# Expert biases as stacked one-pass matmuls, and the scatter of expert rows as a one-hot matmul of gated, split rows

## The chip, the cores and the metric

The kernel runs on one core of a Trainium2 chip. The metric is the time of one execution on the device in microseconds. The core has five engines with instruction streams of their own: TensorE (PE; its weight loads are shown as PEld), VectorE (DVE), ScalarE (ACT), GpSimd (POOL) and SyncE (SP), which here mostly issues DMAs. They meet through semaphores only.

## What is computed

Two transformer blocks, one after the other, on 256 tokens of 1024 channels, all in float32. Only the end of the first block is touched: a mixture of 32 experts, of which each token takes 4. Some 400 of the 486 MB that the kernel moves are expert weights. Cut to what matters:

```python
def moe_ffn(h, w_router, b_router, w1, b1, w2, b2):
    logits = hf @ w_router + b_router
    top_val, top_idx = lax.top_k(logits, TOP_K)        # 4 of 32
    gates = jax.nn.softmax(top_val, axis=-1)
    ...                                                # rows of each expert collected
    def expert_block(args):
        e, tok, g = args
        xb = hf[tok]
        gu = xb @ w1[e] + b1[e]                        # 1024 -> 2048
        gate = jnp.minimum(gu[:, :D_FF], SWIGLU_LIMIT)
        up = jnp.clip(gu[:, D_FF:], -SWIGLU_LIMIT, SWIGLU_LIMIT)
        act = (up + 1.0) * gate * jax.nn.sigmoid(SWIGLU_ALPHA * gate)
        return (act @ w2[e] + b2[e]) * g[:, None]      # 1024 -> 1024, times the gate
    ...                                                # summed back per token
```

## The kernel before, in words

**Stages.** From 0 to about 229 us the first block's mixing and memory attention run (`block_pre`); its weight matmuls (L319) take operands split by ACT (L209, the rounded high part `wh`) and DVE (L210, the rest `wl`). From about 229 to 1212 us the experts run one after the other (`block_moe`). From there `post_head` and the second block take the rest.

**One expert.** Each expert has 64 slots. `gather` (L714) collects the rows of four experts at a time with a one-hot matrix `OG`. `expert_in` then computes 64 x 2048 values as four outputs of 64 x 512 in two PSUM banks, the halves of a bank in the left and right 64 columns of the array. First come four bias matmuls (L741): a one-hot `bs` of 32 rows (L736, DVE) picks row e of the bias table `b1`, whose four quarters lie in four groups of 32 partitions. Then 32 matmuls follow (L746), four for each of eight weight chunks. A float32 matmul is two instructions on the chip. DVE and ACT make the activation (L808 to L812), PE transposes it (L815), ACT copies it out (L817), and 16 matmuls (L829) over four weight chunks make the output `Y`, 64 rows for each half of the channels, which lie in partitions 0 to 63 and 64 to 127.

**Combine.** After every second expert, `combine` adds two experts' rows back to the tokens `x`. `weigh` (L788) has multiplied the one-hot by the gates, so `combine_weights` transposes gated one-hots (L800, copied by ACT at L802), each twice, for the two halves of partitions. `rows_out` copies `Y` to `ysb` (L834, ACT). Eight float32 matmuls with 64 rows each (L845) and four additions by DVE (L848) finish it. For the last two experts `post_head` does the same at L1084, and at L1109 it adds the same product in transposed form to a transposed copy of `x` (L884), which the next block needs.

**Order and buffers.** A scheduler builds each engine's order ahead of time; every engine then runs its list in order. The weights come in 1 MB chunks, issued by SP in the order of use: for each expert eight of `w_expert_in` (L198) and four of `w_expert_out` (L201). Twelve buffers named `w` hold them. SP's next issue waits until PE (or whoever read it last) has released the buffer. At expert 16 (`half`) there is a branch (L868, L869) that handles experts with more than 64 tokens and isn't taken with these inputs; weights for some chunks are loaded ahead of it.

Of the kernel before, what the change touches and what calls it, by code (L numbers as in the profile page):

```python
# [10 lines left out]
F32 = mybir.dt.float32  # L11
F32R = mybir.dt.float32r
# [4 lines left out]
ALU = mybir.AluOpType  # L17
# [25 lines left out]
def host_constants():  # L43
    i = np.arange(P)
    f = np.float32
    c = {}
    c["ident"] = np.eye(P, dtype=f)
    c["ones"] = np.ones((P, P), f)
    c["sbtri"] = -(i[:, None] >= i[None, :]).astype(f)
    c["nones"] = -np.ones((P, P), f)  # L50
    c["neg"] = np.where(i[:, None] >= i[None, :], f(-1e30), f(0))
    c["before"] = (i[:, None] < i[None, :]).astype(f)
    c["iota_e"] = np.tile(np.arange(NE, dtype=f), (P, 1))
    c["iota_s"] = np.tile(np.arange(CAP, dtype=f), (P, 1))
    c["bselc"] = np.concatenate([np.eye(NE, dtype=f)] * 4)
# [12 lines left out]

WIDTH = {"iota_e": NE, "iota_s": CAP, "bselc": NE, "omask": 64}
# [273 lines left out]
def block_pre(K, A):  # L343
# [92 lines left out]
    moe_load(K, A)  # L436
    K.gemm(w_in, 1024, 4, xT, "N", ev_vu, pre=pre_w)
# [140 lines left out]
    ple_load(K, A)  # L578
    ssx2 = K.t([P, 2, 4], F32, "ssx", 2)
# [178 lines left out]
def block_moe(K, A, x):  # L758
# [73 lines left out]
    def rows_out(e):  # L832
        y = K.t([P, 512], F32, "ysb", 3)
        nc.scalar.copy(y, Ys.pop(e))  # L834
        return y

    def combine(e):
        cws = [combine_weights(e - 1), combine_weights(e)]
        ys = [K.yprev, rows_out(e)]
        for tt in range(2):  # L840
            pss = [K.bank("A") for _ in range(2)]
            for i in range(2):
                for h in range(2):
                    pr = slice(64 * h, 64 * h + 64)
                    nc.tensor.matmul(pss[h], cws[i][pr, tt], ys[i][pr], start=i == 0, stop=i == 1)  # L845
            for h in range(2):
                xs = x[:, tt, h * 512:(h + 1) * 512]
                nc.vector.tensor_tensor(xs, pss[h], xs, op=ALU.add)  # L848
# [4 lines left out]
    for e in range(K.nexp):  # L853
# [17 lines left out]
        if prev is not None:  # L871
            gemm2(e - 1, prev, ahead2, range(LAST if last else 0, 4))
# [14 lines left out]
    K.cw, K.Y = cw, Ys[last]  # L887
# [164 lines left out]
def post_head(K, A, x):  # L1052
# [4 lines left out]
    y = K.t([P, 512], F32, "ysb", 3)  # L1057
# [645 lines left out]
def program(tc, A, cst, out, nexp=NE, post=True):  # L1703
    with ExitStack() as ctx:
# [7 lines left out]
        bias_in(K, A)  # L1712
# [67 lines left out]
```

## Time and profile before

| what | us |
|---|---|
| median of 3 runs | 1556.54 |
| lowest and highest | 1555.26, 1558.83 |
| the profiled execution's own time | 1555.18 |
| its span (first to last instruction) | 1553.4 |
| PE busy, share of the span | 1470.1, 95% |
| DVE, ACT, POOL busy | 540.0, 384.1, 53.0 |
| bytes moved by DMA | 486.31 MB |

Busy shares are averages over stages. In the expert stage PE is busy nearly all the time and so is the DMA; in the second block both have gaps. A busy PE here includes weight loads and pipelined ends. PEclk is the clock that was granted to TensorE as a share of 2.4 GHz; 0.5 is 1.2 GHz. The DMA share is the mean of the core's 16 DMA engines.

### The profile page before, as it was taken

The page shows a single profiled execution, that of the slowest core. Times are in us where ns is not written, and L with a number is a line of the kernel's source. Part 1 is how long each engine was busy: PE and PEld are TensorE (multiplying, and loading weights), DVE is VectorE, ACT ScalarE, POOL GpSimd, SP SyncE. Part 2 cuts the span into 40 slices and gives each one's busy share as a digit, 9 for nine tenths or more (in the row PEclk, how much of TensorE's full clock was granted, in tenths as well). Part 3 has the DMA queues.
Part 4 walks back from the last instruction along what each step waited for, and adds up shares of the span by engine and source line. Part 5 has one row for each costly group of instructions (what it writes and reads, how often), then busy time and mean ns, then how long its engine had stood idle before and what let it go on. Part 6 is the DMA issues. An engine that isn't in the chain of part 4 may idle for free.

```text
span 1553.4 us, 20385 instructions
## 1 busy us (share of the span) xinstructions
PE 1470.1 (95%) x8440; PEld 797.7 (51%) x8440; DVE 540.0 (35%) x993; ACT 384.1 (25%) x783; POOL 53.0 (3%) x56
## 2 busy tenths in 40 slices
PE   9999999999999999998999999999999975889998
PEld 7899983332333333332233333223333764878998
DVE  5557652112121111121111111211111655985575
ACT  5845441000010010010001000000000553445654
POOL 0010010000000000000000000000000102500000
PEclk9999999999999999999999999999999997999999
DMA  9694348999999999999999999999998453332463
GB/s 336 218 317 163 119 172 308 418 415 418 417 407 400 410 417 416 416 418 369 382 416 418 410 416 418 415 417 414 388 419 331 140 109 98 109 123 89 153 197 107
DMA packets 146497, 486.31 MB, mean 313 GB/s; under 512 B 8605, under 2 KB 77341, under 8 KB 113504
## 3 DMA queue, kind: packets, MB, share of 16 engines
q1 hardware_dynamic: 143968, 479.10, 79.1%
q0 software_dynamic: 1504, 4.12, 1.5%
q10 hardware_dynamic: 928, 1.74, 0.4%
q8 instruction: 68, 1.11, 0.3%
q14 instruction: 29, 0.24, 0.0%
HBM read 481.78 MB, written 3.15 MB: 312 GB/s over the span
## 4 chain that ended last, share of the span: by engine, by line
PE 38%; issue 7%; DVE 4%; DMA 2%; ACT 2%; POOL 0%; POOLq 0%; ACTq 0%; DVEq 0%
PE pP L746 13%; PE pY L829 9%; PE pA L319 4%; PE pA L845 3%; PE pP L741 3%; DMA w<-in_w_in_dram 2%; DVE t L1375 1%; PE pA L714 1%; PE pY L1320 1%; PE pA L815 1%; DVE t L1376 1%; DVE r L1369 1%; PE pP L1688 0%; PE pA L800 0%; DVE x L848 0%
## 5 line engine op out<-in xcount | busy, mean ns | idle before, releaser
L746 PE MATMUL pP<-w,xg 128*64 128x512 f32 x2024 | 444.0, 594 | 0.0
L746 PEld LDWEIGHTS pP<-w,xg 128*64 128x64 f32 x2024 | 143.2, 137 | 294.4 <-issue 278.7
L829 PE MATMUL pY<-w,hgu 128*64 128x512 f32 x1024 | 279.7, 614 | 4.6 <-PEq L869 4.6
L209 ACT CAST wh<-w 128x512 fp32r<-128x512 f32 (+1 forms) x256 | 155.1, 615 | 157.0 <-PE pA L319 97.4
L210 DVE TENSOR_TENSOR wl<-w,wh 128x512 fp32r<-128x512 f32 x232 | 157.0, 687 | 76.3 <-ACT wh L209 73.2
L808 DVE TENSOR_SCALAR wh<-pP 128x512 f32<-128x512 f32 x32 | 22.1, 691 | 445.4 <-PE pP L746 445.4
L829 PEld LDWEIGHTS pY<-w,hgu 128*64 128x64 f32 x1024 | 71.6, 138 | 160.6 <-issue 145.7
L809 ACT ACTIVATE wh<-wh 128x512 f32<-128x512 f32 x32 | 20.2, 630 | 518.4 <-DVE wh L808 500.0
L319 PE MATMUL pA<-wh,xh 128*128 128x256 f32 x496 | 143.4, 289 | 2.5 <-DVE bk L1346 2.5
L319 PE MATMUL pA<-wh,xl 128*128 128x256 f32 x496 | 142.6, 288 | 0.0
L319 PE MATMUL pA<-wl,xh 128*128 128x256 f32 x496 | 141.5, 285 | 0.0
L319 PE MATMUL pA<-xh,wh 128*128 128x256 f32 x368 | 107.6, 292 | 4.5 <-ACT wh L209 2.3
L319 PE MATMUL pA<-xh,wl 128*128 128x256 f32 x368 | 105.9, 289 | 2.3 <-DVE wl L210 2.3
L319 PE MATMUL pA<-xl,wh 128*128 128x256 f32 x368 | 104.7, 285 | 0.0
L319 PEld LDWEIGHTS pA<-wh,xh 128*128 128x128 f32 x496 | 95.9, 193 | 4.0 <-issue 3.1
L845 PE MATMUL pA<-ysb,cw 64*128 64x512 f32 x240 | 76.5, 654 | 21.5 <-DVE x L848 11.6
L319 PEld LDWEIGHTS pA<-wl,xh 128*128 128x128 f32 x496 | 95.6, 193 | 0.4 <-issue 0.2
L319 PEld LDWEIGHTS pA<-wh,xl 128*128 128x128 f32 x496 | 95.5, 193 | 0.3 <-issue 0.2
L848 DVE TENSOR_TENSOR x<-pA,x 128x512 f32<-128x512 f32 x60 | 38.8, 686 | 153.4 <-PE pA L845 153.4
L741 PE MATMUL pP<-b,bs 32*64 32x512 f32 x256 | 89.5, 617 | 0.0
L319 PEld LDWEIGHTS pA<-xh,wh 128*128 128x128 f32 x368 | 70.5, 192 | 7.7 <-ACT wh L209 3.4
L319 PEld LDWEIGHTS pA<-xh,wl 128*128 128x128 f32 x368 | 70.4, 192 | 3.5 <-DVE wl L210 3.1
(425 smaller groups left out, 1417.5 us busy)
## 6 DMA issues: line engine op xcount, KB each, us to landing
w<-in_w_expert_in_dram SPq DMA_DIRECT2D x253, 1024.0 KB, 11.8
w<-in_w_expert_out_dram SPq DMA_DIRECT2D x128, 1024.0 KB, 10.7
w<-in_w_in_dram SPq DMA_DIRECT2D x31, 1024.0 KB, 5.5
w<-in_w_mem_kv_dram SPq DMA_DIRECT2D x8, 1024.0 KB, 12.0
w<-in_w_out_dram SPq DMA_DIRECT2D x8, 1024.0 KB, 5.6
w<-in_w_mem_q_dram SPq DMA_DIRECT2D x4, 1024.0 KB, 7.0
w<-in_w_mem_o_dram SPq DMA_DIRECT2D x4, 1024.0 KB, 5.3
w<-in_w_ple_gate_dram SPq DMA_DIRECT2D x4, 1024.0 KB, 4.7
```

Of the source, the lines that this page charges most:

```text
L209: nc.scalar.copy(wh, src)
L210: (nc.gpsimd if lo == "P" else nc.vector).tensor_tensor(wl, src, wh.bitcast(F32), op=ALU.subtract)
L319: nc.tensor.matmul(ps[:, j], lh, rh, start=n == 0, stop=n == tot - 1)
L714: nc.tensor.matmul(ps, xx[tt][:, k * P:(k + 1) * P], og[:, tt], start=n == 0, stop=n == 3)
L741: nc.tensor.matmul(out[i], bs[pr], K.b1[pr], start=True, stop=False, tile_position=(32 * i, 64 * (i % 2)))
L746: nc.tensor.matmul(out[i], xs, raw[:, i * 512:(i + 1) * 512], start=False, stop=k == KT - 1)
L808: nc.vector.tensor_scalar(g, Pb[0], 7.0, None, op0=ALU.min)
L809: nc.scalar.activation(sg, g, AF.Sigmoid, scale=1.702)
L815: nc.tensor.transpose(ps[:, j].rearrange("p a b -> p (a b)"), u[:, j * P:(j + 1) * P], c["ident"])
L829: nc.tensor.matmul(Y[64 * h:64 * h + 64], act[:, k % 4, k // 4], raw[:, j * 1024 + h * 512:j * 1024 + h * 512 + 512], start=k == 0, stop=k ...
L845: nc.tensor.matmul(pss[h], cws[i][pr, tt], ys[i][pr], start=i == 0, stop=i == 1)
L848: nc.vector.tensor_tensor(xs, pss[h], xs, op=ALU.add)
```

## The change

Two representations change; the weights' matmuls L746 and L829 stay as they are.

- **Bias.** `b1` becomes 128 rows x 2 x 512 in fp32r: for each of the two PSUM banks, rows 0 to 63 hold the rounded quarters of the bias table and rows 64 to 127 what the rounding left. `bias_in` loads the table twice (eight DMAs instead of four) and is called earlier in the program; the new `bias_split` makes the two parts with two ACT copies and two DVE subtractions. `bs` becomes 128 x 128, still one-hot, and the four bias matmuls of an expert become two, 128 x 128 by 512, one for each bank.
- **Scatter.** `weigh` no longer repeats its result. `combine_weights` transposes the gated one-hot at half the width (64 columns instead of 128), makes a plain one-hot out of it (`is_gt`, DVE) that ACT copies to the upper 64 partitions, and sums up the gates (`reduce_sum`, DVE; copied up by ACT). It is now called for each expert at the place where its `gemm2` begins. `rows_out` no longer copies `Y`: for each half of the channels ACT multiplies it by the gate into one half of the partitions of `st`, rounded to fp32r, and DVE computes what the rounding left into the other half. The eight float32 matmuls with 64 rows become eight fp32r matmuls with 128 rows. `post_head` does the same for the last two experts.

The core of the diff:

```diff
 def bias_in(K, A):
-    b1 = K.b1 = K.m([P, 512], F32, "b1", 1)
-    for i in range(4):
-        nc.scalar.dma_start(b1[32 * i:32 * i + 32], A["b_expert_in"][0][:, 512 * i:512 * i + 512])
+    b1 = K.b1 = K.m([P, 2, 512], F32R, "b1", 1)
+    K.b1raw = [K.m([P, 512], F32, "ohr", 2) for _ in range(2)]
+    for b in range(2):
+        for i in range(4):
+            o = 1024 * b + 512 * (i % 2)
+            nc.scalar.dma_start(K.b1raw[b][32 * i:32 * i + 32], A["b_expert_in"][0][:, o:o + 512])
+def bias_split(K):
+    lo = slice(64, P)
+    for b, raw in enumerate(K.b1raw):
+        nc.scalar.copy(K.b1[:, b], raw)
+        nc.vector.tensor_tensor(K.b1[lo, b], raw[lo], K.b1[lo, b].bitcast(F32), op=ALU.subtract)
 def expert_in(K, A, e, spare={}):
-    for i in range(4):
-        pr = slice(32 * i, 32 * i + 32)
-        nc.tensor.matmul(out[i], bs[pr], K.b1[pr], start=True, stop=False, tile_position=(32 * i, 64 * (i % 2)))
+    for b in range(2):
+        nc.tensor.matmul(Pb[b], bs.rearrange("p j c -> p (j c)"), K.b1[:, b], start=True, stop=False)
     def combine_weights(e):
-        ps = K.bank("A", (P, 2, P))
-        for tt in range(2):
-            nc.tensor.transpose(ps[:, tt], OHG[g][:, tt, j].rearrange("p a b -> p (a b)"), c["ident"])
-        cw = K.t([P, 2, P], F32, "cw", 4)
-        nc.scalar.copy(cw, ps)
-        return cw
+        ps = K.bank("A", (CAP, 2, P))
+        for tt in range(2):
+            nc.tensor.transpose(ps[:, tt], OHG[g][:, tt, j], c["ident"])
+        cw = K.t([P, 2, P], F32R, "cw", 4)
+        gate = K.t([P, 1], F32, "gate", 4)
+        nc.vector.tensor_scalar(cw[0:64], ps, 0.0, None, op0=ALU.is_gt)
+        nc.scalar.copy(cw[64:P], cw[0:64].bitcast(F32))
+        nc.vector.reduce_sum(gate[0:64], ps, axis=AX.XY)
+        nc.scalar.copy(gate[64:P], gate[0:64])
+        return cw, gate
     def combine(e):
-        cws = [combine_weights(e - 1), combine_weights(e)]
-        ys = [K.yprev, rows_out(e)]
-        for tt in range(2):
-            pss = [K.bank("A") for _ in range(2)]
-            for i in range(2):
-                for h in range(2):
-                    pr = slice(64 * h, 64 * h + 64)
-                    nc.tensor.matmul(pss[h], cws[i][pr, tt], ys[i][pr], start=i == 0, stop=i == 1)
+        pair = K.yprev, rows_out(K, Ys.pop(e), cwg.pop(e))
+        for tt in range(2):
             for h in range(2):
+                ps = K.bank("A")
+                for i, (cw, st) in enumerate(pair):
+                    nc.tensor.matmul(ps, cw[:, tt], st[h], start=i == 0, stop=i == 1)
+def rows_out(K, Y, cwg):
+    cw, gate = cwg
+    st = []
+    for h in range(2):
+        t = K.t([P, 512], F32R, "st", NST)
+        a, b = (slice(64 * i, 64 * i + 64) for i in (h, 1 - h))
+        K.nc.scalar.mul(t[a], Y[a], gate[a])
+        K.nc.vector.scalar_tensor_tensor(t[b], Y[a], gate[a], t[a].bitcast(F32), op0=ALU.mult, op1=ALU.subtract)
+        st.append(t)
+    return cw, st
...
 def post_head(K, A, x):
-        nc.scalar.copy(y, K.Y)
-        for j in range(4):
-            for h in range(2):
-                k = 4 * h + j
-                pr = slice(64 * h, 64 * h + 64)
-                for i, yy in enumerate((K.yprev, y)):
-                    mm(K.xT[k // 2][:, k % 2], yy[pr, j * P:(j + 1) * P], K.cw[i][pr].rearrange("p a b -> p (a b)"),
-                       start=False, stop=k % 2 == 1 and i == 1)
+        pair = K.yprev, rows_out(K, K.Y, K.cwg)
+        for k in range(KT):
+            for i, (cw, st) in enumerate(pair):
+                mm(K.xT[k // 2][:, k % 2], st[k // 4][:, k % 4 * P:k % 4 * P + P], cw.rearrange("p a b -> p (a b)"),
+                   start=False, stop=k % 2 == 1 and i == 1)
```

The scheduler also builds another order. The first place is PE at a pair's second expert, between the last L746 (L761 in the changed kernel) of one expert and the first of the next. `pP` are the two banks of `expert_in`, `pY` the output bank, `pA` the banks of the transposes and the combine; a float32 matmul is one row here. Before:

```order
L741 MATMUL pP_5607<-b_397_2522,bs_5605 64x512 [waits DVE_49]
L741 MATMUL pP_5608<-b_397_2522,bs_5605 64x512 [waits DVE_49]
L829 MATMUL pY_5398<-w_5399,hgu_5298 64x512 [waits DMAHW7_49,Activation_49]
L829 MATMUL pY_5398<-w_5399,hgu_5298 64x512 x3
L800 MATMUL pA_5423<-cpack_120,ohw_4620 128x128 x2
L741 MATMUL pP_5608<-b_397_2522,bs_5605 64x512
L845 MATMUL pA_5435<-ysb_5325,cw_5426 128x512 [waits Activation_49]
L829 MATMUL pY_5398<-w_5417,hgu_5298 64x512 [waits DMAHW2_49]
L845 MATMUL pA_5435<-ysb_5433,cw_5431 128x512 [waits Activation_49]
L845 MATMUL pA_5443<-ysb_5325,cw_5426 128x512 [waits DVE_49]
L746 MATMUL pP_5453<-w_5459,xg_4575 64x512 [waits DMAHW3_49]
```

Now:

```order
L756 MATMUL pP_5734<-b_77_484,bs_5732 128x512 [waits DVE_49]
L756 MATMUL pP_5735<-b_77_484,bs_5732 128x512 [waits DVE_49]
L848 MATMUL pY_5520<-w_5521,hgu_5400 64x512 [waits DMAHW3_49,Activation_49]
L815 MATMUL pA_5511<-cpack_120,ohw_4710 64x128 x2
L857 MATMUL pA_5551<-st_5436,cw_5405 128x512 [waits Activation_49]
L857 MATMUL pA_5555<-st_5439,cw_5405 128x512 [waits DVE_49,PE_49]
L761 MATMUL pP_5569<-w_5573,xg_4665 64x512 [waits DMAHW7_49]
L857 MATMUL pA_5551<-st_5545,cw_5514 128x512 [waits DVE_49]
L857 MATMUL pA_5555<-st_5548,cw_5514 128x512 [waits DVE_49]
L857 MATMUL pA_5559<-st_5436,cw_5405 128x512 [waits DVE_49]
L857 MATMUL pA_5563<-st_5439,cw_5405 128x512 [waits DVE_49]
L761 MATMUL pP_5569<-w_5579,xg_4665 64x512 [waits DMAHW0_49]
```

The bias is one piece instead of two, and the last six combine matmuls now stand among the next expert's first four weight matmuls: L761 goes 1, 2, 1 and then 28 in a row, where L746 went 32 in a row behind the whole combine.

The second place is DVE at the same pair's end, where `st` is made and `x` is added to. Before, only the additions stood there:

```order
L736 CAST bs_5827<-cpack_120 128x64 [waits PE_49]
L848 TENSOR_TENSOR x_112<-pA_5435,x_112 128x512 [waits PE_49]
L848 TENSOR_TENSOR x_112<-pA_5436,x_112 128x512 [waits PE_49]
L848 TENSOR_TENSOR x_112<-pA_5443,x_112 128x512 [waits PE_49]
L848 TENSOR_TENSOR x_112<-pA_5444,x_112 128x512 [waits PE_49]
```

Now:

```order
L818 TENSOR_SCALAR cw_5514<-pA_5511 64x256 [waits PE_49]
L820 TENSOR_REDUCE gate_5515<-pA_5511 64x1
L909 SCALAR_TENSOR_TENSOR st_5545<-pY_5520,gate_5515,st_5545 64x512 [waits DVE_49,Activation_49]
L909 SCALAR_TENSOR_TENSOR st_5548<-pY_5520,gate_5515,st_5548 64x512 [waits Activation_49]
L859 TENSOR_TENSOR x_112<-pA_5551,x_112 128x512 [waits PE_49]
L859 TENSOR_TENSOR x_112<-pA_5555,x_112 128x512 [waits PE_49]
```

On ACT `rows_out` was one copy (L834). Before:

```order
L809 ACTIVATE wh_5385<-wh_5383 128x512 [waits DMAHW3_49,DMAHW0_49,DVE_49]
L817 COPY hgu_5396<-pA_5391 128x512 [waits PE_49]
L802 COPY cw_5426<-pA_5423 128x256 [waits PE_49]
L802 COPY cw_5431<-pA_5428 128x256 [waits PE_49]
L834 COPY ysb_5433<-pY_5398 128x512 [waits PE_49,Activation_49]
```

Now:

```order
L828 ACTIVATE wh_6546<-wh_6544 128x512 [waits DVE_49]
L836 COPY hgu_6557<-pA_6552 128x512 [waits PE_49]
L819 CAST cw_6562<-cw_6562 64x256 [waits DVE_49]
L821 COPY gate_6563<-gate_6563 64x1 [waits DVE_49]
L908 ACTIVATE st_6593<-pY_6568,gate_6563 64x512 [waits PE_49]
L908 ACTIVATE st_6596<-pY_6568,gate_6563 64x512 [waits DVE_49]
```

The copy became two multiplications by the gate. The second of them waits for DVE's first L909, so `rows_out` goes ACT, DVE, ACT, DVE, and DVE's one-hot, sum and split rows now come ahead of its additions.

The third place is ACT near the program's start, where the split of the biases is put between casts of the first weight matrix `w_in` (L211 is L209 of before). Before:

```order
L209 CAST wh_277<-w_113 128x512 [waits DVE_49,PE_49]
L209 CAST wh_295<-w_115 128x512 [waits DMAHW4_49,DVE_49,PE_49]
L209 CAST wh_311<-w_115 128x512 [waits DVE_49,PE_49]
L209 CAST wh_327<-w_115 128x512 [waits DVE_49,PE_49]
L209 CAST wh_343<-w_115 128x512 [waits DVE_49,PE_49]
```

Now:

```order
L211 CAST wh_277<-w_113 128x512 [waits DVE_49,PE_49]
L628 DMA ohr_486<-in_b_expert_in_dram 32x512
L211 CAST wh_295<-w_115 128x512 [waits DMAHW5_49,DVE_49,PE_49]
L211 CAST wh_311<-w_115 128x512 [waits DVE_49,PE_49]
L635 CAST b_77_484<-ohr_485 128x512 [waits DMAHW2_49,DMAHW0_49]
L211 CAST wh_327<-w_115 128x512 [waits DVE_49,PE_49]
L635 CAST b_77_484<-ohr_486 128x512 [waits DMAHW6_49,DMAHW7_49,DMAHW4_49,DMAHW1_49]
L211 CAST wh_343<-w_115 128x512 [waits DVE_49,PE_49]
```

The two bias casts stand behind the DMAs that they wait for, and the second of them stands ahead of five casts of `w_in`.

## Rows read from the trace of the kernel before

**Rows 1.** Windows: stretch, length, busy us of PE, PEld, DVE, ACT, POOL, PEclk, DMA, GB/s
```profile
260.00:1190.00 930.00, 901.60 (x3832) 300.09 (x3830) 154.70 (x263) 76.17 (x148) 0.00 (x0) 0.99 1.01 410
590.00:700.00 110.00, 106.97 (x456) 34.68 (x453) 18.50 (x30) 8.76 (x17) 0.00 (x0) 1.00 1.02 417
500.00:510.00 10.00, 10.00 (x49) 3.42 (x50) 0.82 (x2) 0.00 (x0) 0.00 (x0) 1.00 0.95 354
710.00:720.00 10.00, 10.00 (x48) 3.29 (x46) 0.00 (x0) 0.00 (x0) 0.00 (x0) 1.00 0.64 232
750.00:760.00 10.00, 10.00 (x47) 3.21 (x46) 1.29 (x2) 0.00 (x0) 0.00 (x0) 1.00 0.76 293
1110.00:1120.00 10.00, 8.87 (x30) 3.30 (x32) 2.67 (x4) 0.30 (x1) 0.00 (x0) 0.83 0.83 323
```

**Rows 2.** Waits of SP, whole span: engine, line, releaser, us, times, longest
```profile
SPq L198 <- PE pP L746: 403.2, 233, 9.5
SPq L201 <- PE pY L829: 300.4, 107, 10.6
```

**Rows 3.** Chain of waits, four experts: start us, us to the next, what
```profile
750.67 13.88 PE pP L746 x64
764.55 1.86 PE pP L741 x6
766.41 1.00 PE pY L829 x2
...
769.86 1.00 PE pP L741 x2
770.86 5.30 PE pY L829 x24
776.16 13.73 PE pP L746 x64
...
808.52 13.88 PE pP L746 x64
...
871.51 13.88 PE pP L746 x64
```

**Rows 4.** DVE timeline, 776 to 812 us: who holds the banks of the biases
```profile
789.08 0.69 DVE L808 TENSOR_SCALAR wh<-pP 128x512 f32<-128x512 f32 x1 [17.99 <-PE pP L746]
789.94 0.69 DVE L810 TENSOR_SCALAR wh<-pP 128x512 f32<-128x512 f32 x1 [0.17 <-PE pP L746]
```

**Rows 5.** Chain of waits in the second block's head: matmuls in fp32r, 256 columns
```profile
1217.48 1.63 PE pA L1078 x12
```

**Rows 6.** PE timeline, 225 to 300 us: the bias matmuls of an early expert
```profile
278.02 1.09 PE L741 MATMUL pP<-b,bs 32*64 32x512 f32 x8
```

**Rows 7.** Timeline, 728 to 752 us: the end of one combine, PE and DVE
```profile
746.18 1.13 PE L845 MATMUL pA<-ysb,cw 64*128 64x512 f32 x4 [0.74 <-ACT ysb L834]
747.34 1.29 DVE L848 TENSOR_TENSOR x<-pA,x 128x512 f32<-128x512 f32 x2 [10.03 <-PE pA L845]
```

**Rows 8.** SP timeline, 240 to 275 us: DMA issues
```profile
257.85 12.34 SPq L198 DMA_DIRECT2D w<-in_w_expert_in_dram  x8
```

**Rows 9.** DMA view, 1166 to 1206 us, in 40 slices of 1 us
```profile
GB/s 410 426 434 426 410 418 434 426 418 385 422 406 397 414 397 418 401 422 397 410 406 426 397 418 387 340 321 350 106 25 0 0 0 0 69 275 385 316 19 0
```

**Rows 10.** Timeline, 1201.5 to 1216 us: the experts' end and the next head
```profile
1212.16 0.58 ACT L1103 COPY ysb<-pY 128x512 f32<-128x512 f32 x1 [9.51 <-PE pY L829]
...
1212.80 2.96 PE L1109 MATMUL pP<-cw,ysb 64*128 64x256 f32 x24 [0.74 <-ACT ysb L1103]
```

**Rows 11.** ACT timeline, 0 to 60 us: casts of the first weights
```profile
31.24 2.36 ACT L209 CAST wh<-w 128x512 fp32r<-128x512 f32 x4 [3.86 <-DMA w<-in_w_in_dram]
```

**Rows 12.** PE timeline at the branch, and windows (as Rows 1) for the clock
```profile
732.20 1.94 PE L829 MATMUL pY<-w,hgu 128*64 128x512 f32 x2 [4.55 <-PEq L869]
...
220.00:230.00 10.00, 6.59 (x41) 5.42 (x41) 6.80 (x26) 5.70 (x13) 3.25 (x3) 1.00 0.32 105
730.00:740.00 10.00, 7.80 (x16) 2.05 (x16) 1.49 (x3) 0.74 (x2) 0.00 (x0) 0.53 1.00 415
```

More of the change, by code (lines that the diff above doesn't have):

```diff
@@ L54, in host_constants @@
     c["iota_s"] = np.tile(np.arange(CAP, dtype=f), (P, 1))
-    c["bselc"] = np.concatenate([np.eye(NE, dtype=f)] * 4)
+    eye = np.eye(NE, dtype=f)
+    none = np.zeros((NE, NE), f)
+    c["bselc"] = np.block([[eye, none], [none, eye], [eye, none], [none, eye]])
     band = np.zeros((P, 4, 3, P), f)
@@ L436, in block_pre @@
     moe_load(K, A)
+    bias_in(K, A)
     K.gemm(w_in, 1024, 4, xT, "N", ev_vu, pre=pre_w)
@@ L578, in block_pre @@
     ple_load(K, A)
+    bias_split(K)
     ssx2 = K.t([P, 2, 4], F32, "ssx", 2)
@@ L781, in block_moe @@
     OHG = {}
+    cwg = {}
     def weigh(g):
-        ow = K.t([P, 2, 4, 2, CAP], F32, "ohw", 2)
+        ow = K.t([P, 2, 4, CAP], F32, "ohw", 2)
         for tt in range(2):
-            gb = G[:, tt, 4 * g:4 * g + 4, None, None].to_broadcast([P, 4, 2, CAP])
-            og = K.OG[g][:, tt].bitcast(F32)[:, :, None, :].to_broadcast([P, 4, 2, CAP])
-            nc.vector.tensor_tensor(ow[:, tt], og, gb, op=ALU.mult)
+            gb = G[:, tt, 4 * g:4 * g + 4, None].to_broadcast([P, 4, CAP])
+            nc.vector.tensor_tensor(ow[:, tt], K.OG[g][:, tt].bitcast(F32), gb, op=ALU.mult)
         OHG[g] = ow
@@ L830, in gemm2 @@
                                      start=k == 0, stop=k == KT - 1)
[L832 to L835, printed above, removed]
     def combine(e):
-        cws = [combine_weights(e - 1), combine_weights(e)]
-        ys = [K.yprev, rows_out(e)]
+        pair = K.yprev, rows_out(K, Ys.pop(e), cwg.pop(e))
         for tt in range(2):
-            pss = [K.bank("A") for _ in range(2)]
-            for i in range(2):
-                for h in range(2):
-                    pr = slice(64 * h, 64 * h + 64)
-                    nc.tensor.matmul(pss[h], cws[i][pr, tt], ys[i][pr], start=i == 0, stop=i == 1)
             for h in range(2):
+                ps = K.bank("A")
+                for i, (cw, st) in enumerate(pair):
+                    nc.tensor.matmul(ps, cw[:, tt], st[h], start=i == 0, stop=i == 1)
                 xs = x[:, tt, h * 512:(h + 1) * 512]
-                nc.vector.tensor_tensor(xs, pss[h], xs, op=ALU.add)
+                nc.vector.tensor_tensor(xs, ps, xs, op=ALU.add)
     half = K.nexp // 2
@@ L871, in block_moe @@
         if prev is not None:
+            cwg[e - 1] = combine_weights(e - 1)
             gemm2(e - 1, prev, ahead2, range(LAST if last else 0, 4))
@@ L876, in block_moe @@
             else:
-                K.yprev = rows_out(e - 1)
+                K.yprev = rows_out(K, Ys.pop(e - 1), cwg.pop(e - 1))
         prev = act
     last = K.nexp - 1
-    cw = [combine_weights(last - 1), combine_weights(last)]
+    K.cwg = combine_weights(last)
     K.xT = [K.bank("P", (P, 2, T)) for _ in range(4)]
@@ L886, in block_moe @@
     gemm2(last, prev)
-    K.cw, K.Y = cw, Ys[last]
+    K.Y = Ys[last]
+def rows_out(K, Y, cwg):
[8 more added lines that the diff above has]
+    return cw, st
 def dense_rest(K, A, x, xh, xl, pos, G, iota_e, g_f):
@@ L1081, in spread @@
         ps = K.bank("Y")
-        pr = slice(64 * h, 64 * h + 64)
-        for i, yy in enumerate((K.yprev, y)):
-            mm(ps, K.cw[i][pr, tt], yy[pr], start=i == 0, stop=i == 1)
+        for i, (cw, st) in enumerate(pair):
+            mm(ps, cw[:, tt], st[h], start=i == 0, stop=i == 1)
         queue.append((ps, x[:, tt, h * 512:(h + 1) * 512]))
@@ L1102, in post_head @@
     with K.tc.manual_schedule(engines={nc.scalar.engine, nc.vector.engine}):
-        nc.scalar.copy(y, K.Y)
-        for j in range(4):
-            for h in range(2):
-                k = 4 * h + j
-                pr = slice(64 * h, 64 * h + 64)
-                for i, yy in enumerate((K.yprev, y)):
-                    mm(K.xT[k // 2][:, k % 2], yy[pr, j * P:(j + 1) * P], K.cw[i][pr].rearrange("p a b -> p (a b)"),
-                       start=False, stop=k % 2 == 1 and i == 1)
+        pair = K.yprev, rows_out(K, K.Y, K.cwg)
+        for k in range(KT):
+            for i, (cw, st) in enumerate(pair):
+                mm(K.xT[k // 2][:, k % 2], st[k // 4][:, k % 4 * P:k % 4 * P + P], cw.rearrange("p a b -> p (a b)"),
+                   start=False, stop=k % 2 == 1 and i == 1)
         split(0)
@@ L1711, in program @@
         x, lg, finish = block_pre(K, A)
-        bias_in(K, A)
         with route(K, x, lg, finish):
```

9 lines of the change are left out of this document (5 added, 4 removed).

## The prediction

> **What bounds the kernel now.** I read the windows first, because busy shares over the whole span say little. From 260 to 1190 us PE is busy 901.6 of 930 us, and the DMA moves 410 GB/s; in a long quiet stretch (590 to 700) it moves 417 GB/s at a share of 1.02 [rows 1]. Both look full, so the question is which one leads. The waits of SP answer half of it: SP waited 403.2 us for PE's L746 and 300.4 us for its L829 [rows 2], so every chunk is issued when PE gives a buffer back. The chain of waits answers the other half. Four experts, one round of plain, combining, plain with gather, combining, take PE 871.51 - 750.67 = 120.84 us [rows 3]. The DMA needs for their 48 chunks of 1.049 MB, at 417 GB/s, 50.3 / 0.417 = 120.7 us. That is a tie. PE leads only by what it lost elsewhere: after each loss it is behind and cannot catch up, and when it is more than the twelve buffers behind, the DMA runs dry. That is what the windows with 354, 293 and 323 GB/s show [rows 1].
>
> The end shows how far PE is behind. In the slices of 1 us the rate falls from about 400 to under 350 at 1191 and to 106 at 1194, with one chunk of the next stage among the last bytes [rows 9]; so the last expert chunk lands at about 1193. The last expert's output is read at 1212.16 [rows 10]. **PE ends 19 us after the weights were there.**
>
> **The bias, part by part.** Removed are two groups of L741, 1.86 and 1.00 us for each expert [rows 3]. In their place come two one-pass matmuls of 512 columns. Twelve fp32r matmuls of 256 columns take 1.63 us [rows 5], 0.136 each; for 512 I take twice that, 0.27. They must still wait for the same banks: DVE frees the first at 789.77 and the second at 790.63 [rows 4], while PE comes from L746 at 789.89 [rows 3]. So the second ends at about 790.95, 1.1 us after L746. That saves 2.86 - 1.1 = 1.75; the two small transposes that each expert now has cost about 0.25. **A plain expert saves 1.5 us**, with bounds of 0.75 (the new pair takes the 1.86 of the old larger group) and 2.1 (no wait for the bank).
>
> Row tiling is what this part gives up. Here the eight bias instructions of an early expert stand together and take 1.09 us [rows 6], against 2.86 in two pieces later on. The Trainium skill, "TensorEngine Tiling (Array Packing)", section "Theoretical Speedup", says that a contraction of at most 32 rows gains up to four times by tiles side by side; the early expert agrees, the later ones don't. By that rule the old bias was worth 1.09 and the change brings nothing there, so four experts would take 4 x 1.75 = 7.0 us more than I work out below, 119.0, still under the DMA's 120.7, and the first rival would get 0.25. I go by the pieces as they ran.
>
> **The combine, part by part.** A combining expert now takes 808.52 - 776.16 = 32.36 us and a plain one 25.49, so the combine costs 6.87 [rows 3]. Afterwards: eight passes at 0.27, 2.2. Two L761 stand alone between them; a lone float32 matmul takes 1.00 where one of a row takes 5.30 / 12 = 0.44 [rows 3], so 1.1 more. Six more changes between kinds of matmul, at the 0.15 by which two equal groups of L746 differ (13.88 and 13.73), 0.9. Then waits. `rows_out` becomes ACT, DVE, ACT, DVE: ACT takes 0.58 for 512 columns [rows 10], DVE 0.65 (half of 1.29), and a hand-over some 0.1 (PE's wait of 0.74 around the copy) [rows 7], so the first `st` is there 1.4 us and the second 2.8 us after `Y`. Behind L857's wait on PE stand the next expert's weight matmuls, and SP waits for those. But the L761 in between cover most: 1.00 of the first 1.4, and 0.27 + 0.9 of the second, leaving 0.6. The last four wait for DVE's additions; I take the 0.74 that PE waits there now [rows 7]. Sum 2.2 + 1.1 + 0.9 + 1.3 = 5.5, a saving of 1.4. The bounds: 2.7 with no waits, and a loss of 0.9 if the chain and the additions are not covered (3.6 of waits).
>
> **Four experts** save 2 x 1.5 + 2 x (1.5 + 1.4) = 8.8 us: PE needs 112.0, between 107 and 119.6. At every bound that is less than 120.7. **So the DMA becomes the bound, and PE can make up 8.7 us of arrears in each four experts.** The added work elsewhere is beside it: some 2 us on DVE and 1 us on ACT for each expert, engines that are busy 154.7 and 76.2 of 930 us [rows 1].
>
> **What the catch-up is worth.** (a) The DMA no longer runs dry: (417 - 354) / 417 of 10 us is 1.5, the window at 750 gives 3.0, that at 1110 gives 2.25, in all 6.7 us. The 4.4 us at 710 stay, since SP itself stops at the branch there [rows 1]. From the means, (417 - 410) / 417 of 930 is 15.6 us of loss, so up to 4 more lie in small pieces; I don't count them. (b) PE's tail behind the last chunk. What is left then is that chunk's four matmuls, 8 x 0.22 = 1.8, and some arrears from the previous expert's combine and the transposes: 3 to 4 us, I take 3.5 instead of 19, **-15.5**. Ends: 2 (PE waits for the last chunk) and 9 (half the arrears remain).
>
> **The rest.** At the experts' start the first release lets SP go on at 257.85 [rows 8], and ahead of it PE has four groups of bias matmuls of about 1.0 [rows 3, 6] that become a quarter of that; part of it was covered by the gather, so -1.5 (0 to -2.4), which the DMA keeps. At the program's start 0.26 MB more are loaded, 0.6 us, while the DMA is the bound, and ACT does two casts of 0.6 us behind the last bias DMA, ahead of five casts of `w_in`. The cover is the 3.86 us for which ACT waits at 31.24 [rows 11]; +1.0 (0 to +4, when the last bias chunk lands so late that the cover is gone). In `post_head` PE's 2.96 us of L1109 behind a copy [rows 10] become one pass each, but `st` comes at 2.8 instead of 0.64 after `Y`: I take 0 (-2 to +2). After that everything waits for `x` and moves as a whole.
>
> **Sum**: -6.7 - 15.5 - 1.5 + 1.0 = -22.7 on the profiled execution's 1555.18, which is 1532.5. The median of the runs lies 1.36 above that execution, so I predict **1534 us**.
>
> **Rivals.**
> *PE stays the bound* (chance 0.10). The saved matmuls are given back as waits: for that each combine has to wait 4.3 us more than I take, since two of them in four experts must eat 8.7 us. For it speaks that `rows_out` and the additions now form one long chain over three engines; against it, that the whole chain is 2.8 us long and has L761 beside it. Small gains at the start and the end remain: 1552 to 1558, likeliest 1555.
> *The clock falls* (0.07), and the time ends above before. At the branch PE stood idle for 4.55 us, and in the window around it the granted clock is 0.53, the level of 1.2 GHz for nearly all of it; in 220 to 230, with gaps in PE's work too, it stays 1.00 [rows 12]. Once the DMA leads, PE waits for chunks all the time. If it then worked at 1.2 GHz for a share f of its work, four experts would take 112 x (1 + f), and that passes the 120.84 of today at f = 0.08. At f = 0.15 it is 128.8, and over some 7.5 rounds that makes +60 us, less 5 us of the start and end: about 1610. At f = 0.09 it is +9, less 5: about 1560. Against it speaks that it feeds on waits: as soon as PE falls behind, it has no wait left, so the rounds should settle at the DMA's 120.7. The worst that I then see is a fall in the last expert, +5 us, which the range holds. The Trainium skill, "TensorE: Matmul & The Clock Gate", section "HAM oscillation — how this bites in real kernels", describes a kernel that does just that, its clock falling in each wait for DMA between bursts of matmuls; the branch agrees with it, and no row here shows it in the short waits for a chunk.
> *The start is late* (0.08). The last bias DMA lands behind several chunks, ACT and DVE hold the casts of `w_in` for all of 4 us or more, and the catch-up ends at 9 us of tail: -6.7 - 10 + 4 + 2 = -10.7, about 1546.
> *More than I count* (0.10): the 4 us of small pieces, the earlier start and a shorter head: 1524 to 1529.
>
> **How the numbers follow.** My forecast, the DMA as the bound with PE 2 to 9 us behind at the end, has 0.65 and runs from 1528 to 1542. The late start and the larger gain are of the same sign. A measurement of this kernel tells about 0.2% (3.1 us) from no change. Faster: 0.65 + 0.08 + 0.10 = 0.83, plus 0.02 of the first rival, 0.85. Same: 0.07 of the first rival. Slower: 0.07 of the clock and 0.01 of the first. For 8 in 10 the range takes the forecast, the larger gain and most of the late start: 1525 to 1548.
>
> **What would show it.** Right: the starts of L761 over four experts lie about 120.7 apart and PE waits for chunks of `w_expert_in`; SP's waits for L761 and L848 shrink; the windows after 500 hold 417 except at the branch; from the last chunk's landing to the first ACT multiplication of `rows_out` in `post_head` there are 2 to 5 us. The bias pair ends about 1.1 us after L761, and L857's waits sum to about 1.3 us a combine. Wrong: PE without waits for DMA and rounds of 120.8 or more (first rival), PEclk well under 1.00 in many windows (the clock), or a first stage that ends over 3 us later. The number is wrong too if the second block does not move along as a whole.

## The result

The changed kernel takes **1531.83 us** (median of 4 runs, 1531.24 to 1534.87) beside 1555.9 of the kernel before in the same job: a ratio of **0.985** (95% interval 0.983 to 0.987). The forecast was 1534, with a range of 1525 to 1548. The profiled execution has a span of 1529.5 us, 23.9 less than before.

The windows of the changed kernel, with the columns of [rows 1]:

```profile
260.00:1170.00 910.00, 850.95 (x3546) 288.50 (x3544) 215.84 (x383) 105.60 (x208) 0.00 (x0) 1.00 1.01 414
500.00:510.00 10.00, 10.00 (x48) 3.52 (x46) 2.15 (x5) 1.79 (x4) 0.00 (x0) 1.00 1.03 423
710.00:720.00 10.00, 7.75 (x32) 2.30 (x28) 1.91 (x5) 1.11 (x3) 0.00 (x0) 1.00 0.65 242
730.00:740.00 10.00, 8.61 (x40) 2.26 (x34) 0.00 (x0) 0.00 (x0) 0.00 (x0) 1.00 1.01 413
750.00:760.00 10.00, 8.33 (x35) 1.94 (x32) 1.50 (x2) 1.36 (x2) 0.00 (x0) 1.00 1.01 421
880.00:890.00 10.00, 7.77 (x34) 1.94 (x32) 0.00 (x0) 0.00 (x0) 0.00 (x0) 1.00 1.01 418
1110.00:1120.00 10.00, 8.89 (x40) 2.74 (x38) 1.55 (x3) 1.64 (x4) 0.00 (x0) 1.00 1.02 422
```

PE now has gaps (7.77 us of 10 in a stretch of L761 alone), and the windows that held 354, 293 and 323 GB/s in [rows 1] hold 421 to 423. Only the stop at the branch is still there, 242 at 710. The waits of SP over the whole span (engine and line, whom it waited for, us, times, longest) changed hands:

```profile
SPq L203 <- DMA w<-in_w_expert_in_dram: 223.1, 113, 3.2
SPq L200 <- DMA w<-in_w_expert_out_dram: 213.3, 109, 3.3
SPq L200 <- PE pP L761: 138.2, 86, 7.2
...
SPq L203 <- PE pP L761: 46.4, 26, 4.2
```

In [rows 2] SP waited 403.2 and 300.4 us for PE to give buffers back. Now it mostly waits for an earlier transfer to land, and for PE's L761 only 138.2 + 46.4 = 184.6. (SP's waits for DVE's `wl`, of the other stages' weight matmuls, are left out: some 310 us in either kernel.) The chain of waits (start, us, what) runs through the transfers:

```profile
800.85 1.96 PE pP L761 x8
...
841.24 19.90 DMA w<-in_w_expert_in_dram
861.22 20.10 DMA w<-in_w_expert_in_dram
881.38 20.14 DMA w<-in_w_expert_out_dram
901.58 19.90 DMA w<-in_w_expert_in_dram
921.52 1.96 PE pP L761 x8
```

Where [rows 3] was PE throughout, five sixths of a round of four experts are now DMA pieces of about 20 us; the first 20 us, of which one line is shown, run over PE's work of one expert. The round takes 921.52 - 800.85 = 120.67 us: the DMA's 120.7. The next one, with two DMA pieces of 21.05 and 20.57 us in it, takes 122.28. So a round is hardly shorter than PE's 120.84 of before: what the change gains is the DMA's dry stretches and PE's tail at the end. The end, from the timeline (answering to [rows 10]; a bracket holds the us for which the engine stood idle before, and whom it waited for):

```profile
1183.12 5.37 PE L848 MATMUL pY<-w,hgu 128*64 128x512 f32 x24
1188.54 0.68 ACT L908 ACTIVATE st<-pY,gate 64x512 fp32r<-64x512 f32 x1 [6.93 <-PE pY L848]
1189.26 0.74 DVE L909 SCALAR_TENSOR_TENSOR st<-pY,gate,st 64x512 fp32r<-64x512 f32 x1 [6.85 <-ACT st L908]
1190.04 0.68 ACT L908 ACTIVATE st<-pY,gate 64x512 fp32r<-64x512 f32 x1 [0.81 <-DVE st L909]
1191.56 1.65 PE L1128 MATMUL pP<-cw,st 128*128 128x256 f32 x6 [0.30 <-DVE st L909]
```

`Y` is read at 1188.54 instead of 1212.16. The last expert chunk lands at 1184.93 (before: 1193.18, both from the transfers' own records), so PE's tail behind it fell from 19.0 to 3.6 us. From the first read of `Y` to the end of the program it is 341.0 us, before 341.2.

### The profile page after: what moved, and what is told of

Read it like the earlier page. It is cut to its first block, busy times and chain, and to the rows that moved or that the text cites. A ratio compares the mean times of both kernels' runs of the same rounds, so it can differ in the third digit from the quotient of the medians.

```text
span 1529.5 us, 19893 instructions
## 1 busy us (share of the span) xinstructions
PE 1414.1 (92%) x8104; PEld 788.1 (52%) x8104; DVE 606.0 (40%) x1123; ACT 416.4 (27%) x849; POOL 53.0 (3%) x56
## 4 chain that ended last, share of the span: by engine, by line
DMA 25%; PE 15%; issue 7%; DVE 5%; ACT 2%; POOL 0%; POOLq 0%; SPq 0%; DVEq 0%; ACTq 0%
DMA w<-in_w_expert_in_dram 14%; DMA w<-in_w_expert_out_dram 8%; PE pA L321 4%; PE pY L848 4%; PE pP L761 2%; DMA w<-in_w_in_dram 2%; DVE t L1394 2%; PE pA L730 1%; DVE t L1395 1%; PE pY L1339 1%; DVE r L1388 1%; PE pP L1707 0%; ACT wh L211 0%; PE pP L896 0%; DVE wl L212 0%
## 5 line engine op out<-in xcount | busy, mean ns | idle before, releaser
L761 PE MATMUL pP<-w,xg 128*64 128x512 f32 x2024 | 487.9, 598 | 37.5 <-DMA w<-in_w_expert_in_dram 37.2
L761 PEld LDWEIGHTS pP<-w,xg 128*64 128x64 f32 x2024 | 142.7, 136 | 342.0 <-issue 231.9
L848 PE MATMUL pY<-w,hgu 128*64 128x512 f32 x1024 | 281.1, 606 | 1.2 <-DMA w<-in_w_expert_out_dram 1.2
L211 ACT CAST wh<-w 128x512 fp32r<-128x512 f32 (+1 forms) x256 | 155.1, 615 | 158.1 <-PE pA L321 99.3
L848 PEld LDWEIGHTS pY<-w,hgu 128*64 128x64 f32 x1024 | 74.5, 136 | 127.4 <-issue 115.7
L909 DVE SCALAR_TENSOR_TENSOR st<-pY,gate,st 64x512 fp32r<-64x512 f32 x64 | 48.0, 750 | 195.2 <-ACT st L908 195.1
L908 ACT ACTIVATE st<-pY,gate 64x512 fp32r<-64x512 f32 x64 | 43.7, 682 | 187.6 <-PE pY L848 161.4
L321 PEld LDWEIGHTS pA<-xl,wh 128*128 128x128 f32 x368 | 71.8, 195 | 0.4 <-issue 0.2
```

What stands on the lines that cost most here:

```text
L211: nc.scalar.copy(wh, src)
L321: nc.tensor.matmul(ps[:, j], lh, rh, start=n == 0, stop=n == tot - 1)
L761: nc.tensor.matmul(out[i], xs, raw[:, i * 512:(i + 1) * 512], start=False, stop=k == KT - 1)
L848: nc.tensor.matmul(Y[64 * h:64 * h + 64], act[:, k % 4, k // 4], raw[:, j * 1024 + h * 512:j * 1024 + h * 512 + 512], start=k == 0, stop=k ...
L908: K.nc.scalar.mul(t[a], Y[a], gate[a])
L909: K.nc.vector.scalar_tensor_tensor(t[b], Y[a], gate[a], t[a].bitcast(F32), op0=ALU.mult, op1=ALU.subtract)
```

## The experiments

My theory: PE and the DMA were tied at 120.8 and 120.7 us a round, the change takes PE below the DMA, and from then on only the DMA's time counts. The main rival: the gain is in proportion to the PE work saved. A second one: it came from the branch, or from TensorE's clock, alone.

### One part at a time

`bias_only` is the kernel before with the bias hunks, and one line to make room:

```diff
-        cw = K.t([P, 2, P], F32, "cw", 4)
+        cw = K.t([P, 2, P], F32, "cw", 2)
```

> The kernel before with the bias part alone (stacked table, two one-pass matmuls, its split at the start); the combine is the old one, its buffer for the combine weights cut from four to two to make room for the larger table. Theory (a tie of PE and DMA, of which PE now falls below): the bias group went from 2.86 to 1.29 us, so four experts take PE 120.84 - 4 x 1.57 = 114.6, under the DMA's 120.7; PE catches up 6 us a round, and nearly the whole gain is there: 1533 to 1538. Rival (the gain goes by the PE work that is saved, 6.3 of some 9.7 us in four experts): two thirds of 24, about 1540 to 1543.

Measured: 1535.19 us (1534.0 to 1536.18), ratio 0.986 (0.981 to 0.991).

`scatter_only` is the changed kernel with the old bias:

```diff
-    for b in range(2):
-        nc.tensor.matmul(Pb[b], bs.rearrange("p j c -> p (j c)"), K.b1[:, b], start=True, stop=False)
+    for i in range(4):
+        pr = slice(32 * i, 32 * i + 32)
+        nc.tensor.matmul(out[i], bs[pr], K.b1[pr], start=True, stop=False, tile_position=(32 * i, 64 * (i % 2)))
```

> The changed kernel with the old bias part (four float32 bias matmuls of 32 rows, four loads of the table), so the scatter alone. Theory: it saves some 3.4 us of PE in four experts, 117.4 is still under 120.7, the arrears of the branch (about 10 us) are made up in three rounds, and the start loses nothing: 1532 to 1539, so both parts alone give most of the gain and together not their sum. Rival (by the work saved, a third of 24): about 1547 to 1549.

Measured: 1531.70 us (1529.06 to 1537.47), ratio 0.985 (0.979 to 0.990). **Each part alone gives nearly the whole gain.** That is what a floor looks like: 24 us for both, 24 for one and 28 for the other (before 1559.55 in this job, with runs from 1547.27 to 1562.94). For `scatter_only` the rival's 1547 to 1549 is excluded. For `bias_only` all four runs lie under the rival's 1540, but the interval of the ratio, wide from the runs of the kernel before, still holds two thirds of the gain (0.990). The transfers' own records settle it: from the 32nd expert chunk's landing to the last one's it takes 893.0 us in the changed kernel, 893.3 in `bias_only`, 892.6 in `scatter_only`, and 901.5 before. What `bias_only` lacks is at the end: PE's tail behind the last chunk is 7.6 us there, and 3.6 in the changed kernel.

### How much work PE has to spare

`dose5` and `dose9` run the bias pair five and nine times:

```diff
+    reps = 5
+    for r in range(reps):
         for b in range(2):
-            nc.tensor.matmul(Pb[b], bs.rearrange("p j c -> p (j c)"), K.b1[:, b], start=True, stop=False)
+            nc.tensor.matmul(Pb[b], bs.rearrange("p j c -> p (j c)"), K.b1[:, b], start=True, stop=r < reps - 1)
```

> The changed kernel with each expert's bias pair run five times over (the first four results are overwritten): 8 passes more, 8 x 0.22 = 1.76 us of PE in each expert. Theory: four experts take PE 111.1 + 7.0 = 118.1, still under 120.7, so the time hardly moves: 1532 to 1537. Rival (by the PE work): 7.0 of the 9.7 us are given back, about 1549.

Measured: 1536.11 us (1535.06 to 1537.87). From the 32nd chunk's landing to the last one's it takes 894.5 us, 1.5 more than in the changed kernel.

> The same with the bias pair run nine times over: 16 passes more, 3.5 us in each expert. Theory: PE needs 111.1 + 14.1 = 125.2 for four experts, leads again, and each of 7.7 rounds costs 4.4 us more than in the kernel before: 1580 to 1592. Rival (by the PE work, 14.1 / 9.7 of 24 us on top of the changed kernel): about 1567.

Measured: 1598.03 us (1597.77 to 1598.98), ratio 1.027. The same step of eight passes an expert costs 4 us the first time (beside 1531.83, from the other job) and 62 the second. The windows from 590 to 700 us of the two, `dose5` first, columns as in [rows 1]:

```profile
590.00:700.00 110.00, 108.57 (x471) 40.82 (x468) 27.57 (x49) 12.85 (x26) 0.00 (x0) 1.00 1.02 416
```

```profile
590.00:700.00 110.00, 109.28 (x468) 42.93 (x465) 25.00 (x45) 12.86 (x26) 0.00 (x0) 1.00 1.00 398
```

With five the DMA still runs at 416 GB/s and PE is busy 98.7%; with nine the DMA starves at 398. The chain of `dose9`:

```profile
842.04 12.17 PE pP L763 x56
...
968.41 12.17 PE pP L763 x56
```

The round is 126.37 us, with no DMA piece in it: PE, but for some 1.5 us of ACT and DVE in each combine. Over 7.7 rounds that is 5.53 x 7.7 = 43 us more than the kernel before, 1598 from 1555.9 or 1602 from the 1559.55 of this job. I had expected 1580 to 1592, so this was missed: I took 0.22 us for a pass, and 64 passes more made the round, PE's 111.1 in the changed kernel (120.84 less the 9.7 worked out below), longer by (126.37 - 111.1) / 64 = 0.24 each. In a row six of them take 1.60, 0.27; that some fill waits that PE had anyway would fit, but isn't shown. The threshold lies between the doses, where it should.

### Taking work away from the floor

`no_combine` leaves out, for all pairs but the first and the last, the gated rows of the second expert, the eight passes and the additions:

```diff
-            if (e - 1) % 2 == 1:
+            if (e - 1) % 2 == 1 and e > 2:
+                Ys.pop(e - 1), cwg.pop(e - 1)
+            elif (e - 1) % 2 == 1:
                 combine(e - 1)
```

> The changed kernel without the combine of all pairs but the first and the last: for those, the gated rows, their eight passes and the four additions are left out. That takes about 10 us of PE out of four experts. Theory: the DMA is the floor already, so the time stays within 2 us: 1529 to 1533. Rival (PE's work still counts, at 24 us for 9.7 us in four experts as the change seemed to give): about 1507.

Measured: 1531.35 us (1530.89 to 1532.01). In the window from 590 to 700 PE is busy 95.3 us instead of the changed kernel's 101.5, and the DMA moves the same 417 GB/s. The changed kernel first, then `no_combine`:

```profile
590.00:700.00 110.00, 101.52 (x425) 34.24 (x426) 25.92 (x47) 13.57 (x27) 0.00 (x0) 1.00 1.02 417
```

```profile
590.00:700.00 110.00, 95.30 (x410) 30.86 (x410) 17.78 (x35) 10.84 (x23) 0.00 (x0) 1.00 1.02 417
```

The combine is free now: a further saving of PE work in the rounds is worth nothing. (The last pair's combine, behind the last chunk, is still in, so this says nothing of the tail.)

### Arrears

`stall17` repeats the bias pair 36 times at one expert, 70 passes more (the loop is that of `dose5`):

```diff
+    reps = 36 if e == 18 else 1
```

> The changed kernel with 70 more one-pass bias matmuls at one expert, the nineteenth (overwritten): some 18 us of PE work in one place, about the arrears that the kernel before had at its end. Theory: PE makes it up at 9 to 10 us in four experts over the 13 experts that are left, and twelve buffers cover the DMA meanwhile, all but what goes beyond them: 1531 to 1536. Rival (arrears are not made up): 1549.

Measured: 1531.33 us (1529.13 to 1536.21). The passes of L758 alone by windows (length, PE, PEld, PEclk, DMA share, GB/s):

```profile
700.00:720.00 20.00, 4.09 (x14) 2.83 (x14) 0.91 0.82 324
720.00:740.00 20.00, 7.52 (x26) 4.38 (x25) 1.00 1.01 415
740.00:760.00 20.00, 8.58 (x31) 5.43 (x31) 1.00 1.02 418
760.00:780.00 20.00, 1.47 (x4) 0.67 (x4) 1.00 1.02 415
```

Nearly 22 us of passes, most of them in 50 us, and the DMA goes on at 415 to 418 (324 is the stop at the branch). The last expert chunk lands at 1183.11, and `Y` is read here:

```profile
1186.67 0.68 ACT L910 ACTIVATE st<-pY,gate 64x512 fp32r<-64x512 f32 x1 [6.92 <-PE pY L850]
```

The tail is 3.6 us, as without the passes: PE made up as much as its whole tail of before.

### The branch

`before_nobranch` and `after_nobranch` leave out the branch, in either kernel:

```diff
-            cnt = nc.values_load(K.cmi[0:1, 0:1], min_val=0, max_val=T)
-            with K.tc.If(cnt > CAP):
-                dense_rest(K, A, x, xh, xl, pos, G, iota_e, g_f)
```

> The kernel before without its branch at expert 16 (the handler for experts with more than 64 tokens, which these inputs don't take, is left out). It prices what PE's arrears of the branch were worth there: PE's idle 4.55 us, about 4.7 us of work at half clock behind it. Theory (PE leads in the kernel before, so its own losses count one to one, and the DMA's lost 4.4 us at SP's stop don't): the experts end some 9 us earlier, 1545 to 1550. Rival (the change gained by the branch alone, since PE's clock no longer falls there in the changed kernel): nearly all of the 24 us, 1533 to 1537.

Measured: 1547.94 us (1543.25 to 1552.51), ratio 0.996 (0.993 to 0.998).

> The changed kernel without the same branch. Theory (the DMA leads, so only what the DMA loses counts): SP no longer stops, the 4.4 us without transfers at 710 to 720 go, PE's own waits there don't matter: 1526.5 to 1528.5. Rival (PE's losses at the branch still reach the end): 1521 to 1524.

Measured: 1529.10 us (1526.7 to 1529.56) beside 1531.83 of the changed kernel in its own job. So the branch is worth about 7 us where PE leads (1555.08 to 1547.94) and 3 where the DMA leads, and the change isn't the branch alone. Both runs have a remainder; `after_nobranch` misses its 1526.5 to 1528.5 by 0.6. Without the branch the DMA's stop is gone (420 GB/s at 710 to 720), but the last expert chunk lands 2.4 us earlier, not 4.4: at the 208th chunk the lead is 3.7, at the 232nd 2.5, from the 304th to the 328th 3.6 again and at the end 2.4. What makes these steps is open. And the profiled execution of `before_nobranch` lost something early, at the first biases of the expert stage:

```profile
231.22 1.97 PE L741 MATMUL pP<-b,bs 32*64 32x512 f32 x2
235.12 1.97 PE L741 MATMUL pP<-b,bs 32*64 32x512 f32 x4
```

Such a group takes 1.00 us at full clock in [rows 3]; here PE worked at 1.2 GHz (granted clock 0.51 from 230 to 240) after a gap of 2.04 us, and the 16th expert chunk landed at 252.94 instead of 245.94. That differs between executions of one kernel: from 230 to 240 us the granted clock was 0.83 in the changed kernel's first profile and 0.92 in its second, and with the same gap it stayed at 1.00 in the kernel before and in `scatter_only`. It may be part of the spread of all runs here: of the twelve runs of the kernel before in this job, the four longest (1557.98 to 1562.76 us) have mean granted clocks of 0.976 to 0.978, the others 0.979 to 0.982. Which way the cause goes wasn't tried.

The two records also say what the branch cost. From the 32nd chunk's landing to the last one's, `before_nobranch` takes 888.8 us (before 901.5) and `after_nobranch` 890.1: without the branch the old kernel's DMA runs as steadily as the new one's. But its tail is still 18.9 us (1187.85 to 1206.70), against 3.6. So in this profile the branch accounts for the dry stretches and not for the tail, which the change takes away without the branch too; its loss of 7 us at the start may be in that tail.

### The start

In `four_loads` the table is loaded once, and DVE writes the low part into the other 64 partitions:

```diff
     for b in range(2):
-        for i in range(4):
-            o = 1024 * b + 512 * (i % 2)
+        for i in range(2):
+            o = 1024 * b + 512 * i
...
-        nc.scalar.copy(K.b1[:, b], raw)
-        nc.vector.tensor_tensor(K.b1[lo, b], raw[lo], K.b1[lo, b].bitcast(F32), op=ALU.subtract)
+        nc.scalar.copy(K.b1[hi, b], raw[hi])
+        nc.vector.tensor_tensor(K.b1[lo, b], raw[hi], K.b1[hi, b].bitcast(F32), op=ALU.subtract)
```

> The changed kernel with the table of biases loaded once (four DMAs, as before) and the low part computed by DVE out of the first 64 partitions into the other 64. It tells which part of the start's +2.0 us (one DMA by GpSimd behind the routing is issued at 233.33 instead of 231.29) is the four more loads. If the loads and the waits behind them are the cost: that DMA is issued at 231.3 to 231.8 and the time falls by about 1.5 to 2 against the changed kernel, 1529 to 1530.5. If the two casts and two subtractions themselves are: it stays at 233, 1531 to 1532.

> The scatter alone once more, beside the changed kernel on the same chip. With the DMA as the floor of both, what is left between them is the start: 0.4 us of delay here against 2.0, and PE with less room to spare here. Expected within 2 us of the changed kernel, at or under it.

> The changed kernel itself on the same chip as the two others, as their yardstick: 1531 to 1533.

Measured in one job: `four_loads` **1528.93** (1526.41 to 1529.24), the scatter alone 1533.04 (1529.72 to 1538.04), the changed kernel 1532.38 (1529.87 to 1534.22), before 1554.88. GpSimd's DMA behind the routing, in the timelines of before, of the changed kernel and of `four_loads`:

```profile
231.29 0.74 POOL L1049 DMA_DIRECT2D e<-KTm  x1 [2.93 <-ACT KTm L1047]
```

```profile
233.33 0.74 POOL L1073 DMA_DIRECT2D e<-KTm  x1 [2.94 <-ACT KTm L1071]
```

```profile
230.22 0.74 POOL L1073 DMA_DIRECT2D e<-KTm  x1 [2.93 <-ACT KTm L1071]
```

The expectation had 231.3 to 231.8 and 1529 to 1530.5; both came out a little lower. In the changed kernel of this job the same DMA came at 235.07, so 1.7 us are scatter between executions, and the profiled execution of `four_loads` is the fastest of its five (1526.41). All profiles together still part the two: in the eight with eight loads this DMA is issued between 232.63 and 235.88, in the five with four loads between 230.22 and 232.16. So the loads and what waits behind them were the cost of the start; the casts and subtractions are not, since they are all still there in `four_loads`. `four_loads` beats both kernels, by 1.7% and 0.2%; the ranges of the two don't meet (1529.24 and 1529.87), though barely. The scatter alone isn't better than the changed kernel, although its start loses only 0.2 to 0.4 us (231.51 here): three of its six runs take 1529.72 to 1529.88 and three 1536.21 to 1538.04, so its median lies where no run does. Why is open. PE has less to spare there (busy 108.58 of the 110 us from 590 to 700 in its first profile), but in `dose5` it has as little (108.57), and its runs lie within 3 us.

## Why the prediction was right

Term by term, in the profiled executions, with the steps of the sum:

| step | forecast | measured |
|---|---|---|
| start | +1.0 | +2.0 (the routing's DMA, 231.29 to 233.33) |
| first release | -1.5 | -1.8 (the 32nd expert chunk lands at 291.96, before at 291.72: 0.2 later, where the start alone would make it 2.0) |
| DMA no longer dry | -6.7 | -8.5 (from the 32nd expert chunk's landing to the last one's 893.0 instead of 901.5) |
| PE's tail | -15.5 | -15.4 (3.6 instead of 19.0) |
| after `Y` | 0 | -0.2 |
| sum | -22.7 | -23.9 |

The sum is closer than its terms: the loss at the start was forecast 1.0 too small and the gain from the dry stretches 1.8, and the two errors partly cancel. The first two rows are also known only together. In the second profile of the changed kernel the routing's DMA comes 3.8 us later than before, which by itself passes the prediction's sign of being wrong (over 3 us), but the 32nd chunk lands only 0.6 later (292.34). Forecast for the two together was -0.5, measured +0.2 and +0.6. The gain of the second row also falls earlier than at the 257.85 that the prediction names: in the first profile the 15th chunk lands 2.6 us later than before, the 16th 0.1.

**The bound.** The step on which all hung, that the two are tied and that PE falls below the DMA, held: the rounds are 120.67 and 122.28, SP's waits moved from PE to the transfers, and the doses put the threshold between 8 and 16 more passes an expert. The proof that the prediction gave for the tie was weaker than it looks. Its 417 GB/s come from a stretch in which PE set the pace, and 50.3 MB in PE's own 120.84 us are 416.5 GB/s, whatever the DMA could do. Only the DMA share of 1.02 spoke for a limit of the DMA itself. That it is one is shown by the changed kernel and by `no_combine`: PE has time to spare, and the rate is still 417.

**The prices on PE.** The timeline of one plain and the next, combining expert:

```profile
863.05 0.49 PE L756 MATMUL pP<-b,bs 128*128 128x512 f32 x1
863.91 0.49 PE L756 MATMUL pP<-b,bs 128*128 128x512 f32 x1 [0.36 <-DVE wh L829]
864.34 1.93 PE L848 MATMUL pY<-w,hgu 128*64 128x512 f32 x6
...
893.21 0.51 PE L756 MATMUL pP<-b,bs 128*128 128x512 f32 x1
...
904.37 1.02 PE L761 MATMUL pP<-w,xg 128*64 128x512 f32 x2
906.11 0.49 PE L857 MATMUL pA<-st,cw 128*128 128x512 f32 x1 [0.71 <-DVE st L909]
906.53 1.08 PE L761 MATMUL pP<-w,xg 128*64 128x512 f32 x4
907.61 0.49 PE L857 MATMUL pA<-st,cw 128*128 128x512 f32 x1
908.04 1.07 PE L761 MATMUL pP<-w,xg 128*64 128x512 f32 x2
909.04 1.20 PE L857 MATMUL pA<-st,cw 128*128 128x512 f32 x4
910.16 10.79 PE L761 MATMUL pP<-w,xg 128*64 128x512 f32 x48
```

The bias takes 864.34 - 863.05 = 1.29 us (forecast 1.1), with the wait for DVE's release that the forecast named. From the bias to the next expert's L761 a plain expert takes 10.2 us (863.05 to about 873.3, where L848 ends) instead of 11.6, so it saves 1.4 (forecast 1.5). The combining one takes 910.16 - 893.21 = 16.95, less 1.77 for the eight L761 instructions in it, 15.2, instead of 808.52 - 789.89 = 18.6: 3.4 (forecast 2.9). The waits in this combine are the one of 0.71 behind DVE's first `st`; the second `st` and the additions are covered. I had put 1.3 there. A round saves 9.7, not 8.8.

**The start** was under-sized: 2.0 against 1.0, inside its bounds of 0 and 4. The fifth transfer of `w_in` landed at 18.78 instead of 17.05, and of the 3.86 us of cover in [rows 11] nothing was used up: ACT still waits 3.84 there, since the transfer it waits for came 1.1 us later itself. The cover was a wait for the very queue that was being delayed.

**The DMA's dry stretches** were under-sized too: worth 8.5, of which I had named 6.7 and left up to 4 uncounted.

**The rivals.** PE as the bound fell with the round and the doses. The clock: PE now stands idle about 0.55 us in each 2.5, and in that window (880 to 890 above) the granted clock is 1.00. What the Trainium skill describes in "TensorE: Matmul & The Clock Gate", section "HAM oscillation — how this bites in real kernels", a clock that falls in each wait for DMA between bursts, this kernel doesn't show in waits of that size. Falls it did show after a gap of 2.04 us at the experts' start and around the branch, in some executions and not in others. The Trainium skill's rule on row tiling ("TensorEngine Tiling (Array Packing)", "Theoretical Speedup") didn't decide either: with the bias part worth nothing the DMA would still have been the bound, as `scatter_only` shows.

## What to carry to other kernels

Work out the round of each resource in the same unit before costing an edit. Where two are as close as here (120.84 and 120.7 us), the first few per cent taken off the leading one give back all arrears that have piled up, and the rest gives nothing; so do the cheaper of two edits. A rate read where another resource sets the pace is not yet the limit of the one that is read: look for a run in which the other has time to spare. A wait that is to cover new work covers it only if it does not hang on the resource that the work loads.

## What the runs showed that I had not expected

PE's stop at the branch goes with when PE gets there. It was 4.55 us before [rows 12], and in the changed kernel:

```profile
714.77 0.38 PE L815 MATMUL pA<-cpack,ohw 128*64 128x128 f32 x2 [1.80 <-PEq L880]
```

In the kernels where PE came late, with SP's transfers under way again, it was 4.8 and 5.1 us (`dose9`, `dose5`); where PE came while the transfers stood still or were just starting again, 2.0 to 2.6 us (`no_combine`, `four_loads`, `bias_only`, `stall17`, `scatter_only`). The scatter alone shows both, in its first profile and in its second, where PE came 1.4 us later and, by the transfers' records, they had been back for some 2 us:

```profile
718.21 0.38 PE L801 MATMUL pA<-cpack,ohw 128*64 128x128 f32 x2 [2.64 <-PEq L866]
```

```profile
721.91 0.61 PE L801 MATMUL pA<-cpack,ohw 128*64 128x128 f32 x2 [4.89 <-PEq L866]
```

Why the transfers should matter to a branch is open. With the stop of 1.80 us the clock did not fall: it is 1.00 from 710 to 720 and from 730 to 740 in the windows above, where [rows 12] show 0.53 behind the stop. In the second profile of the changed kernel, with a stop of 2.04 us, it did, for a shorter time than before:

```profile
710.00:720.00 10.00, 7.96 (x26) 2.34 (x26) 2.29 (x7) 1.11 (x3) 0.00 (x0) 0.83 0.65 236
```
